# A two-layer float32 block on one Trainium2 core: the low part of every fourth pair of weight blocks formed by an accumulating DMA instead of VectorE

## Chip, cores and metric

One Trainium2 chip, one core of it. The metric is the device time of one execution in microseconds (us), lower is better.

## What is computed

Two transformer layers on 256 tokens of width 2048, everything in float32. Layer 1 is a hybrid mixer (an indexed sparse attention with 8 heads and a block attention with 8 heads, merged by two sigmoid gates), a cross attention to 256 memory rows, and a SwiGLU feed-forward of width 5632, each followed by residual and layer norm. Layer 2 has three attention branches of 4 heads (forgetting, chunked with relative positions, stick breaking), each with a silu gate, an up-projection and a sigmoid gate of width 2048, and an output product. By far the most of the work is the products with weight matrices:

```
x = layer_norm(ALPHA * x + hybrid_mixer(x, ...), ...)
x = layer_norm(ALPHA * x + mem_cross_attention(x, mem, ...), ...)
x = layer_norm(ALPHA * x + swiglu(x, w_ffn_in, w_ffn_out), ...)
x = hybrid_layer(x, norm_g, w_in, ...)      # layer 2
```

## The kernel before

**Products.** TensorE multiplies float32r operands, a form with a shorter mantissa. To keep float32 results, every operand is written as a sum of two parts, hi and lo, and three products are summed: hi by hi, hi by lo, lo by hi (`mm3`, L121 to L126: L124 and L126 read the weight's hi, L125 its lo). The activations, transposed, are the stationary operand (128 x 128), the weights the moving one (128 x 512).

**Weights.** `load_w` (L105 to L119) brings the weights in as pairs of blocks of 128 rows: a tile `raw` of 128 x 2 x 512 float32 (512 KB) by a DMA of SyncE's queue (L112), then `split` (L100 to L102): ScalarE copies raw into `hi` with a cast to float32r (L101), VectorE subtracts hi from raw into `lo` (L102).

```
    def split(src, hi, lo):
        nc.scalar.copy(hi, src)
        nc.vector.tensor_sub(lo, src, hi.bitcast(F32))
```

`raw`, `hi` and `lo` come from three rings of six buffers each (N_R = 6 and N_W = 6). So the cast of a pair waits until TensorE has read the pair six places before it, and the load of a pair until VectorE (and ScalarE) have read the raw six places before. 760 pairs go through `load_w`. The first 24 are those of the indexer queries (w_qi, 16) and of the narrow panel w_misc (8, 336 columns). All later ones have 512 columns, and every product takes a multiple of eight pairs, or four in w_oa, w_ob, w_up and each of the two halves of w_kvm for the values of the memory.

**Order of the products.** `gemm_panels` (L128 to L150) goes block by block over k: for each block both token tiles, three matmuls each, so 12 matmuls per pair. Where a layer norm follows (w_out, w_omem, the last group of w_fo) and in the last product (w_out2), the last TAIL = 8 blocks (four pairs) go token tile by token tile: first all eight blocks for tile 0, then all eight for tile 1. After a layer norm (w_qmem, the first w_fi, the first w_qkvg) the first HEAD = 8 blocks do the same.

**Other work on the engines involved.** ScalarE also evacuates PSUM, does exponentials, sigmoids and squares. VectorE also does layer norms (`layer_norm_T`, L528 to L548), softmax pieces, gates and `ln_affine` (L550 to L559), which multiplies and adds rows of gain and offset to x. GpSimd (POOL) makes a few masks at the start and issues the DMAs of its own queue: broadcast rows of 512 columns into tiles `bb` (three buffers, `bias_tile`, L95 to L98, issued at L93), x itself (L501), the relative-position tables (L799, L800) and some small constants. The framework plans the order on each engine by costs of its own, so an engine's order is not the order of the text: three `bb` loads and the small constants stand at the start of POOL's queue, for instance. Once planned, each engine and each queue goes in order.

Of the kernel before, what the change touches and what calls it, by code (L numbers as in the profile page):

```python
# [11 lines left out]
OP = mybir.AluOpType  # L12
# [20 lines left out]
N_EARLY2 = 2  # L33
E1 = 1

# columns of w_in
C_QD, C_KV, C_QI, C_KI, C_WI, C_QM, C_KM, C_VM, C_GA, C_GB = (
# [3 lines left out]
def build(ctx, tc, nc, a):  # L41
# [27 lines left out]

# [1 line left out]
    ident = const.tile([128, 128], F32, name="ident")  # L71
# [4 lines left out]
    nc.vector.memset(eps6, EPS)  # L76
    # token tile 1 sees 256 keys; the tables of tile 0 are the right halves of its
    dist1 = const.tile([128, 256], F32, name="dist1")
# [21 lines left out]
    def split(src, hi, lo):  # L100
        nc.scalar.copy(hi, src)  # L101
        nc.vector.tensor_sub(lo, src, hi.bitcast(F32))  # L102

# [1 line left out]
    def load_w(chunk_ap, kn, n, pieces=1):  # L105
        """One chunk of weights: kn blocks of 128 rows, n columns; hi and lo parts of each."""
        parts = []
        for k0 in range(0, kn, 2):
            raw = raws.tile([128, 2, n], F32, name="raw", tag="raw")
            for i in range(pieces):  # L110
                q = slice(2 * i // pieces, 2 * (i + 1) // pieces)
                nc.sync.dma_start(raw[:, q, :], chunk_ap[:, k0 + q.start:k0 + q.stop, :])  # L112
            hi = his.tile([128, 2, n], F32R, name="hi", tag="hi")
            lo = los.tile([128, 2, n], F32R, name="lo", tag="lo")
            for i in range(pieces):
                q = slice(2 * i // pieces, 2 * (i + 1) // pieces)
                split(raw[:, q, :], hi[:, q, :], lo[:, q, :])
            parts += [(hi[:, i, :], lo[:, i, :]) for i in range(2)]
        return parts  # L119
# [8 lines left out]
    def gemm_panels(panels, n=512, head=0, tail=0):  # L128
        """panels: (w_ap, acts, evac) each; acts: list over k of (hi, lo) [128, 256];
        w_ap: [chunks, 128, 4 * n]. The first `head` and the last `tail` blocks of 128 rows  # L130
        go token tile by token tile, the others block by block."""
        items = [(p, k) for p, (_, acts, _) in enumerate(panels) for k in range(len(acts))]
        cut = len(items) - tail
        groups = ([items[:head]] if head else []) + [[i] for i in items[head:cut]] + ([items[cut:]] if tail else [])
        pss, w = {}, {}
        for g in groups:
            for p, k in g:
                if (p, k) not in w:
                    ap = panels[p][0]
                    for i, part in enumerate(load_w(ap[k // 4].rearrange("p (k n) -> p k n", n=n), 4, n)):  # L140
                        w[p, k + i] = part
            for tt in range(2):
                for p, k in g:
                    _, acts, evac = panels[p]
                    if (p, tt) not in pss:
                        pss[p, tt] = ps_g.tile([128, 512], F32, name="ps_g", tag="ps_g")[:, :n]
                    last = k == len(acts) - 1
                    mm3(pss[p, tt], acts[k], w[p, k], tt, k == 0, last)
                    if last:
                        evac(tt, pss[p, tt])  # L150
# [10 lines left out]
    def transpose4(src):  # L161
        """src [128, 512] -> PSUM [128, 4, 128], each block of 128 columns transposed."""
        pt = ps_t.tile([128, 4, 128], F32, name="ps_t", tag="ps_t")
        for i in range(4):
            nc.tensor.transpose(pt[:, i, :], src[:, i * 128:(i + 1) * 128], ident)  # L165
        return pt
# [26 lines left out]

# [1 line left out]
    def scores(q, k, tt, w):  # L195
# [20 lines left out]
    def weigh(ps, v, causal_keys=True):  # L216
        """ps: per token tile [128, 2, 256]; v(i, sc) -> [128 keys, 128]. PSUM [128, 2, 256] = out^T."""
        o = ps_a.tile([128, 2, 256], F32, name="ps_a", tag="ps_a")
# [16 lines left out]

    # =========================== layer 1: mixer ===========================
    def stream_parts(src, name, panels, first=False):
        """Products with src^T (256 columns) that is loaded chunk by chunk beside the weights:
        a function that does the chunks from c0 to c1."""
        pss, loaded = {}, {}  # L240
# [6 lines left out]
        def part(c0, c1):  # L247
            for c in range(c0, c1):
                w0 = {}

                def first_w(i):
                    # between the pieces of src^T: blocks 2 i' and 2 i' + 1 of the first panel
                    if i % 2 == 0:
                        ap = panels[0][0][c].rearrange("p (k n) -> p k n", n=512)
                        w0[i // 2] = load_w(ap[:, i:i + 2, :], 2, 512, 2)
# [27 lines left out]
    def warm(func, after):  # L283
        """Has the function's table loaded once `after` is there, before it is needed."""
        nc.scalar.activation(small([128, 1], "warm"), after, func, bias=eps5, scale=0.0)
# [69 lines left out]

    # keys of the memory
    kmemT = unit([128, 4, 256], F32, "kmemT")
    stream(a["memT"], "memT", [(a["w_kvm"][0], into_T(kmemT))])

    # indexer scores and the choice of 64 keys  # L360
    mdsa = []
    for tt in range(2):
        w = 128 * (tt + 1)
        acc = later(f"score{tt}", FLOOR, tt=tt)
        for bp in range(4):
            # blocks 2 bp, 2 bp + 1 of two heads each; the heads of one row half share a bank
            for half in range(2):
# [20 lines left out]

    # keys and values of the latent attention, per head
    def load_pairs(ap):  # L390
# [111 lines left out]

    # residual + layer norm
    stats = {}
# [14 lines left out]

    # gains and offsets of the layer norms with one column per block of 128 of x's columns  # L520
    def columns(name):
# [6 lines left out]
    def layer_norm_T(g, b, prs, warm_up):  # L528
        """For a token tile: x becomes (x - mean) / deviation; prs get its transpose with gain and offset."""
        def ln(tt):  # L530
# [19 lines left out]
    def ln_affine(i, then=None):  # L550
        """Gain and offset on x itself."""
        for j in range(4):
# [8 lines left out]
    mA = acts_of(mT)  # L561
    # values of the memory: the first chunks run beside the layer norm
    vmem = unit([128, 2, 512], F32, "vmem")
# [5 lines left out]

    # =========================== memory attention ===========================  # L570
    v_part(0, V_CUT)
# [29 lines left out]

    # =========================== feed forward ===========================
    x2A = acts_of(x2T)
# [41 lines left out]

    # The rms norm's factor of a token, r3, is a factor of the token's rows of all products with
    # w_in_2: it comes in after them. hn here is x3 norm_g.

    # =========================== layer 2 ===========================
    hA = acts_of(hnT)  # L650
# [4 lines left out]

    # the branch gates of the first branch; its rows wait for r3
    first = []
# [16 lines left out]

    # silu of the branch gates, transposed
    sgT = []
# [14 lines left out]

    # log of the forget gates and its running sum
    fraw = const.tile([128, 16, 4], F32, name="fraw")
# [20 lines left out]
    nc.scalar.activation(fe, fe, AF.Exp)  # L714
    # log(1 + e) = log(u) e / (u - 1) with u = 1 + e rounded, and e where u = 1
    nc.vector.tensor_scalar(fu, fe, 1.0, None, op0=OP.add)
# [56 lines left out]

    # branch a: forgetting attention
    qT = proj_norm_T(a["w_qkvg"][0, 0], 0)
# [20 lines left out]

    # branch b: chunked attention with relative positions
    rb = [unit([128, 4, 128 * (tt + 1)], F32, f"rb{tt}") for tt in range(2)]
# [21 lines left out]

    # branch c: stick breaking
    qT2 = proj_T(a["w_qkvg"][2, 0], hA, sc=r3)
# [16 lines left out]
    for tt in range(2):  # L839
# [4 lines left out]
        for h in range(4):  # L844
            # softplus(z), then its sum over this key and the later ones
            nc.vector.scalar_tensor_tensor(e[:, h, :], z[:, h, :], 0.0, e[:, h, :], op0=OP.max, op1=OP.add)
            sr = tmp([128, 256], "scan")
            nc.vector.tensor_tensor_scan(sr[:, 0:w], e[:, h, ::-1], e[:, h, ::-1], 0.0, OP.add, OP.bypass)
            nc.vector.tensor_sub(z[:, h, :], z[:, h, :], sr[:, w - 1::-1] if w == 256 else sr[:, 127::-1])
    # gates and up-projections  # L850
    def gate2(n, j):
# [40 lines left out]

# [1 line left out]
def _panels(w, n=512, kc=4):  # L894
    """[K, N] -> [N / n, K / (128 kc), 128, kc * n]"""
    k, m = w.shape
# [4 lines left out]
def _lay_out(i):  # L901
# [13 lines left out]
    o["w_gb"] = _panels(w[:, C_GB:])  # L915
    # [h, d, c] -> [128 c, 2, (h d)];  [h, c, d] -> [128 c, 2, (h d)]
    o["w_ukT"] = np.ascontiguousarray(f["w_uk"][0].reshape(8, 128, 2, 128).transpose(3, 2, 0, 1)).reshape(128, 2, 1024)
# [45 lines left out]
```

## Time and profile before

| | us |
|---|---|
| span of the profiled execution, first to last instruction | 2244.9 |
| median of the timed runs | 2246.86 (two: 2244.22 and 2249.5) |
| TensorE busy | 2217.8 (99%) |
| VectorE busy | 1278.9 (57%) |
| ScalarE busy | 1056.4 (47%) |
| GpSimd busy | 36.8 (2%) |
| DMA, mean rate | 189 GB/s |

The page gives the profiled execution's span, not its time as the other runs are timed. The median of the timed runs is 1.96 us above the span. A busy TensorE in this profile means that a matmul was under way; matmuls overlap, so a row's mean duration is longer than the step from one matmul to the next.

### The profile page before, as it was taken

How to read it: one execution, taken by the hardware profiler on the slowest of the kernel's cores; microseconds unless marked ns; L12 is line 12 of the kernel's file. 1: busy time of each engine (PE TensorE's matmuls, PEld its weight loads, DVE VectorE, ACT ScalarE, POOL GpSimd, SP SyncE). 2: the span in 40 equal slices, each digit the busy share in tenths (PEclk: the TensorE clock that was granted, in tenths of full speed). 3: DMA queues.
4: the chain of work that ended last, by engine and by line, in shares of the span. 5: the costliest groups of instructions: out<-in, count | busy, mean ns of one | idle time of the engine just before them, and what ended most of it. 6: DMA issues, size and time to landing. Idle time of an engine off the chain costs nothing.

```text
span 2244.9 us, 26525 instructions
## 1 busy us (share of the span) xinstructions
PE 2217.8 (99%) x10080; PEld 1819.9 (81%) x10080; DVE 1278.9 (57%) x1563; ACT 1056.4 (47%) x1327; POOL 36.8 (2%) x75
## 2 busy tenths in 40 slices
PE   8999999999999999999999999999999999999999
PEld 6788888888887788888888888887788888888887
DVE  5666455555558774454455545467565565655553
ACT  5655445444435554443344434446555554444442
POOL 1000000000000000000000000001000000000000
PEclk9999999999999999999999999999999999999999
DMA  7654555656766375555555556557455556666563
GB/s 275 206 166 144 183 174 171 200 194 199 249 196 197 132 236 191 191 188 192 193 188 188 190 194 194 187 173 229 144 173 175 165 169 203 197 204 199 191 201 115
DMA packets 118480, 423.96 MB, mean 189 GB/s; under 512 B 13728, under 2 KB 14288, under 8 KB 118352
## 3 DMA queue, kind: packets, MB, share of 16 engines
q1 hardware_dynamic: 113760, 407.59, 55.2%
q0 software_dynamic: 4592, 14.68, 2.4%
q8 instruction: 79, 1.29, 0.2%
q14 instruction: 49, 0.40, 0.1%
HBM read 420.11 MB, written 2.10 MB: 188 GB/s over the span
## 4 chain that ended last, share of the span: by engine, by line
issue 66%; PE 30%; DMA 2%; POOL 1%; DVE 1%; ACT 0%; POOLq 0%; DVEq 0%; ACTq 0%
PE ps_g L125 9%; PE ps_g L126 9%; PE ps_g L124 9%; DMA bb<-ln_b 1%; PE ps_t L165 1%; DMA bb<-ln_g 1%; POOL bb L93 0%; DMA bb<-b_gate 0%; PE ps_a L198 0%; PE ps_a L232 0%; DVE lo L102 0%; PE ps_a L233 0%; ACT tmp L298 0%; PE ps_t L221 0%; PE ps_a L741 0%
## 5 line engine op out<-in xcount | busy, mean ns | idle before, releaser
L102 DVE TENSOR_TENSOR lo<-raw,hi 128x1024 fp32r<-128x1024 f32 (+2 forms) x766 | 931.7, 1218 | 874.7 <-ACT hi L101 873.7
L101 ACT CAST hi<-raw 128x1024 fp32r<-128x1024 f32 (+2 forms) x766 | 802.5, 1049 | 1038.4 <-PE ps_g L126 995.9
L125 PE MATMUL ps_g<-lo,hnTh 128*128 128x512 f32 x768 | 301.8, 393 | 2.3 <-DVE lo L102 2.3
L126 PE MATMUL ps_g<-hi,hnTl 128*128 128x512 f32 x768 | 302.1, 393 | 0.0
L124 PE MATMUL ps_g<-hi,hnTh 128*128 128x512 f32 x768 | 302.1, 393 | 0.0
L124 PE MATMUL ps_g<-hi,x2Th 128*128 128x512 f32 x704 | 275.0, 391 | 0.0
L126 PE MATMUL ps_g<-hi,x2Tl 128*128 128x512 f32 x704 | 274.8, 390 | 0.0
L125 PE MATMUL ps_g<-lo,x2Th 128*128 128x512 f32 x704 | 274.2, 390 | 0.0
L124 PE MATMUL ps_g<-hi,xTh 128*128 128x512 f32 (+1 forms) x608 | 236.5, 389 | 6.2 <-ACT hi L101 6.2
L125 PE MATMUL ps_g<-lo,xTh 128*128 128x512 f32 (+1 forms) x608 | 236.9, 390 | 1.5 <-DVE lo L102 1.3
L126 PE MATMUL ps_g<-hi,xTl 128*128 128x512 f32 (+1 forms) x608 | 237.8, 391 | 0.0
L125 PEld LDWEIGHTS ps_g<-lo,hnTh 128*128 128x128 f32 x768 | 145.1, 189 | 32.3 <-DVE lo L102 2.7
L124 PEld LDWEIGHTS ps_g<-hi,hnTh 128*128 128x128 f32 x768 | 145.2, 189 | 29.7 <-ACT crow L742 0.3
L126 PEld LDWEIGHTS ps_g<-hi,hnTl 128*128 128x128 f32 x768 | 144.9, 189 | 29.5
L125 PEld LDWEIGHTS ps_g<-lo,x2Th 128*128 128x128 f32 x704 | 132.2, 188 | 27.3 <-DVE lo L102 0.2
L124 PEld LDWEIGHTS ps_g<-hi,x2Th 128*128 128x128 f32 x704 | 132.2, 188 | 27.2 <-DVE x2Th L546 0.2
L126 PEld LDWEIGHTS ps_g<-hi,x2Tl 128*128 128x128 f32 x704 | 132.2, 188 | 27.1
L124 PEld LDWEIGHTS ps_g<-hi,xTh 128*128 128x128 f32 x608 | 114.7, 189 | 28.9 <-ACT hi L101 6.9
L126 PE MATMUL ps_g<-hi,hTl 128*128 128x512 f32 x352 | 137.3, 390 | 0.0
L124 PE MATMUL ps_g<-hi,hTh 128*128 128x512 f32 x352 | 137.2, 390 | 0.0
L125 PE MATMUL ps_g<-lo,hTh 128*128 128x512 f32 x352 | 136.9, 389 | 0.0
L125 PEld LDWEIGHTS ps_g<-lo,xTh 128*128 128x128 f32 x608 | 114.6, 188 | 25.6 <-DVE lo L102 3.4
(325 smaller groups left out, 2403.3 us busy)
## 6 DMA issues: line engine op xcount, KB each, us to landing
raw<-w_fi SPq DMA_DIRECT2D x176, 512.0 KB, 4.1
raw<-w_qkvg SPq DMA_DIRECT2D x96, 512.0 KB, 3.7
raw<-w_g SPq DMA_DIRECT2D x96, 512.0 KB, 4.4
raw<-w_fo SPq DMA_DIRECT2D x88, 512.0 KB, 3.7
raw<-w_out SPq DMA_DIRECT2D x64, 512.0 KB, 4.5
raw<-w_ga SPq DMA_DIRECT2D x32, 512.0 KB, 4.7
raw<-w_gb SPq DMA_DIRECT2D x32, 512.0 KB, 4.6
raw<-w_up SPq DMA_DIRECT2D x24, 512.0 KB, 4.6
```

The costliest lines, as they stand in the source:

```text
L101: nc.scalar.copy(hi, src)
L102: nc.vector.tensor_sub(lo, src, hi.bitcast(F32))
L124: nc.tensor.matmul(ps, ah[:, tok(tt)], wh, start=first, stop=False)
L125: nc.tensor.matmul(ps, ah[:, tok(tt)], wl, start=False, stop=False)
L126: nc.tensor.matmul(ps, al[:, tok(tt)], wh, start=False, stop=last)
L165: nc.tensor.transpose(pt[:, i, :], src[:, i * 128:(i + 1) * 128], ident)
```

## The change

A constant DMA_LO = 4 and a second way to split are added. From the 25th pair on, every fourth pair that `load_w` loads in one piece with 512 columns takes it: ScalarE copies raw into hi as before, then writes the negated raw, rounded to float32r, into lo, and a DMA of GpSimd's queue adds raw onto lo in place. VectorE has no part in such a pair. The pairs meant are those numbered 28, 32, ..., 760: (760 - 28) / 4 + 1 = 184 of them. The pairs are still counted over all of `load_w`; the activations' splits are as before. The diff also takes out comments and docstrings, which is left out here.

```
+DMA_LO = 4
...
+    pairs_done = [0]
+
+    def split_dma(src, hi, lo):
+
+        nc.scalar.copy(hi, src)
+        nc.scalar.mul(lo, src, -1.0)
+        nc.gpsimd.dma_start(lo, src, accum_op=OP.add)
+
     def load_w(chunk_ap, kn, n, pieces=1):
...
             hi = his.tile([128, 2, n], F32R, name="hi", tag="hi")
             lo = los.tile([128, 2, n], F32R, name="lo", tag="lo")
+            pairs_done[0] += 1
+            by_dma = pieces == 1 and n == 512 and pairs_done[0] > 24 and pairs_done[0] % DMA_LO == 0
             for i in range(pieces):
                 q = slice(2 * i // pieces, 2 * (i + 1) // pieces)
-                split(raw[:, q, :], hi[:, q, :], lo[:, q, :])
+                (split_dma if by_dma else split)(raw[:, q, :], hi[:, q, :], lo[:, q, :])
```

## Rows read from the trace of the kernel before

**Rows 1.** The page: busy time of each engine, TensorE's granted clock by slices.

```profile
PE 2217.8 (99%) x10080; PEld 1819.9 (81%) x10080; DVE 1278.9 (57%) x1563; ACT 1056.4 (47%) x1327; POOL 36.8 (2%) x75
...
PEclk9999999999999999999999999999999999999999
```

**Rows 2.** Windows: stretch, its us, busy per engine (instructions), clock, DMA share, GB/s.

```profile
0.00:100.00 100.00, 89.10 (x423) 72.84 (x423) 57.75 (x85) 58.34 (x85) 9.19 (x26) 1.00 0.77 263
100.00:200.00 100.00, 98.99 (x500) 80.25 (x500) 72.94 (x167) 55.69 (x98) 0.00 (x0) 1.00 0.45 144
700.00:800.00 100.00, 92.36 (x414) 73.57 (x413) 77.40 (x122) 57.00 (x99) 5.48 (x10) 0.97 0.53 170
900.00:950.00 50.00, 50.00 (x226) 41.39 (x225) 24.45 (x22) 21.15 (x23) 0.00 (x0) 1.00 0.60 189
1500.00:1550.00 50.00, 47.27 (x217) 37.48 (x216) 40.92 (x69) 35.58 (x72) 7.51 (x12) 0.97 0.58 177
1550.00:1700.00 150.00, 149.23 (x697) 119.46 (x696) 83.03 (x118) 79.34 (x109) 0.00 (x0) 0.99 0.51 174
```

**Rows 3.** Waits of TensorE: who waited for whom, us in total, times, longest.

```profile
PE ps_g L124 <- ACT hi L101: 6.2, 2, 5.3
PE ps_a L198 <- ACT prob L584: 3.8, 1, 3.8
PE ps_g L125 <- DVE lo L102: 3.6, 4, 2.3
```

**Rows 4.** Groups by line and shape: busy us, mean ns, idle before and its releaser.

```profile
L102 DVE TENSOR_TENSOR lo<-raw,hi 128x1024 fp32r<-128x1024 f32 x754 | 921.8, 1224 | 856.6 <-ACT hi L101 855.5
L101 ACT CAST hi<-raw 128x1024 fp32r<-128x1024 f32 x754 | 794.0, 1055 | 1026.4 <-PE ps_g L126 989.4 <-issue 8.6 <-ACT g L871 8.2
...
L871 ACT ACTIVATE g<-g 128x1024 f32<-128x1024 f32 x12 | 12.6, 1053 | 0.0
```

**Rows 5.** Timeline in the feed-forward, one pair: start us, us, engine, line, operation.

```profile
1005.07 0.39 PE L124 MATMUL ps_g<-hi,hTh 128*128 128x512 f32 x1
...
1005.27 1.05 ACT L101 CAST hi<-raw 128x1024 fp32r<-128x1024 f32 x1 [1.50 <-PE ps_g L126]
1005.30 0.39 PE L125 MATMUL ps_g<-lo,hTh 128*128 128x512 f32 x1
...
1006.36 1.23 DVE L102 TENSOR_TENSOR lo<-raw,hi 128x1024 fp32r<-128x1024 f32 x1 [1.28 <-ACT hi L101]
...
1007.99 1.05 ACT L101 CAST hi<-raw 128x1024 fp32r<-128x1024 f32 x1 [1.67 <-PE ps_g L126]
```

**Rows 6.** GpSimd's loads of x at L501: issue time of one in ns, landing.

```profile
L501 POOL DMA_DIRECT2D x<-x x4: 530/533/536, 575.9 to 577.5; - x4
...
DMA to landing us min/median/max: 8.1/11.1/14.2
```

**Rows 7.** GpSimd's broadcast rows at L93 (256 KB each): landing, all of them.

```profile
DMA to landing us min/median/max: 3.5/5.2/10.7
```

**Rows 8.** The page: DMA queues (packets, MB, share of 16 engines' span), one kind of issue.

```profile
q1 hardware_dynamic: 113760, 407.59, 55.2%
q0 software_dynamic: 4592, 14.68, 2.4%
...
raw<-w_fi SPq DMA_DIRECT2D x176, 512.0 KB, 4.1
```

**Rows 9.** Waits of SyncE's queue: us in total, times, longest.

```profile
SPq L112 <- DVE lo L102: 1706.0, 713, 10.4
```

**Rows 10.** Timeline at the end: the last pair's cast, the last matmul.

```profile
2224.58 1.05 ACT L101 CAST hi<-raw 128x1024 fp32r<-128x1024 f32 x1 [1.67 <-PE ps_g L126]
...
2240.47 0.39 PE L126 MATMUL ps_g<-hi,mT2l 128*128 128x512 f32 x1
```

**Rows 11.** Timeline of GpSimd in an `ln_affine` and in layer 2's gates.

```profile
799.60 0.54 POOL L93 DMA_DIRECT2D bb<-ln_g  x1 [8.27 <-DVE x L557]
...
2065.89 0.54 POOL L93 DMA_DIRECT2D bb<-b_gate  x1 [26.66 <-DVE g L467]
```

## Prediction

> **What bounds the kernel now.** I read the page's busy times first. TensorE is busy for 2217.8 of 2244.9 us, at a granted clock of nine tenths or more in each of the 40 slices, while VectorE has 1278.9 and ScalarE 1056.4 [rows 1]. All the time in which TensorE does nothing is therefore 2244.9 - 2217.8 = 27.1 us, 1.2% of the span. That is the most that faster work on any other engine could return, and it is under 2%, which is about what a measurement of this kernel can tell from no change.
>
> Then I looked at where the 27.1 us lie, by windows. 10.9 stand in the first 100 us, 1.0 in the next, 7.6 around the memory attention (700 to 800), 2.7 and 0.8 around layer 2's start; the 4.1 that are left are the evacuation and store after the last matmul. In the feed-forward (900 to 950) TensorE is never idle [rows 2]. Its waits name ScalarE's cast (6.2 us) and softmax (3.8) before VectorE's subtraction (3.6) [rows 3].
>
> Last the two engines that feed TensorE. VectorE's subtraction of a pair takes 1224 ns and ScalarE's cast 1055 ns; the idle time before the cast, 989.4 us of it, ends with L126, that is with TensorE giving a buffer back [rows 4]. Both are ahead of TensorE and wait for it. The timeline shows how far ahead: casts start at 1005.27 and 1007.99, so a pair takes 2.72 us and a matmul 2.72 / 12 = 0.227; TensorE starts the next pair at 1005.07 as the cast begins; VectorE starts its subtraction 0.04 us after the cast ends [rows 5]. With six buffers, five pairs lie between the cast of a pair and its first matmul: 5 x 2.72 = 13.6 us. The lo part is needed one matmul later, at 13.8, and is there after 1.05 + 0.04 + 1.23 = 2.3. It has 11.5 us in hand.
>
> **The change part by part.**
>
> *Removed from VectorE:* 184 subtractions of 1.224 us, 225 us of its busy time [rows 4]. In the steady stretches VectorE waits for casts that wait for TensorE, so this returns nothing there. What it can return lies where TensorE idles after the 24th pair: 1.0 + 7.6 + 2.7 + 0.8 = about 12 us at the very most [rows 2], of which only a part waits for VectorE.
>
> *Added to ScalarE:* 184 multiplications 128 x 1024 from SBUF to SBUF. The trace has the same form in the sigmoid on g, 1053 ns, and the cast, 1055 [rows 4]; I take 1.05. That is 193 us more, 1056 to about 1250, 56% of the span. In a steady stretch four pairs last 10.9 us and ScalarE would have 5 x 1.05 = 5.3 of casts and multiplications in them; the cover is its wait for TensorE. Where TensorE waits for ScalarE each multiplication could cost its full 1.05. The idle stretches after pair 24 (100 to 200, 700 to 800, 1500 to 1700) are 400 us long and hold 400 / 10.9 = 37 such pairs, so 39 us at most. With the 12 us from VectorE the net is between -12 and +39. As a multiplication only matters where it stands just before a waited-for instruction, and each takes an equally long subtraction off VectorE, I take +2.
>
> *Added to GpSimd and the DMA engines:* 184 issues and as many accumulating transfers of 512 KB within SBUF. No row shows one. Call L the time from GpSimd's issue to the landing. The lo part of such a pair is then ready at 1.05 + 1.05 + 0.04 + L after the start of the cast, and must be there at 13.8: **L may be 11.7 us** before TensorE waits in a steady stretch. The nearest rows are GpSimd's loads of x, also 512 KB in rows of 4 KB: 8.1, median 11.1, 14.2, where the four were issued within 1.6 us, so that only the 8.1 had nothing of its own queue ahead of it [rows 6]. Half the size takes 3.5 to 10.7, median 5.2 [rows 7]; on SyncE's queue 512 KB take 4.1 [rows 8]. The ends are 3.5 and 14.2; I take 8.1, the row of equal size with an empty queue. It leaves 3.6 us.
>
> *Where the lead is shorter:* in the four tails the last four pairs are needed at half the distance. At the end the last cast starts at 2224.58; the tail is 48 matmuls of 0.227 before 2240.9, so it starts at 2230.0, and the last pair's lo is needed 18 + 1 matmuls later, at 2234.3 [rows 10]. L may be 2234.3 - 2224.58 - 2.14 = 7.6 us there. All panels hold four or eight pairs, so the last pair of each tail has a number divisible by four and goes by DMA. At L = 8.1 each tail waits 0.5 us: 4 x 0.5 = 2. In the three heads the eighth pair gets the second's buffer after 8.2 of the head's 10.9 us and may take L = 9.0: no cost.
>
> *Moved: the release of raw.* SyncE's loads now wait for VectorE's subtraction, 1706 us in 713 waits, so they too are issued as early as a buffer comes free [rows 9]. After the change every fourth buffer is free only at 2.14 + 8.1 = 10.2 us after its cast began, not 2.3. The next load into it lands 4.1 later [rows 8], at 14.3, and its cast is due at 6 x 2.72 = 16.3: 2 us to spare. The three loads queued behind it in SyncE's order start late as well, in a bunch; TensorE would see a late cast only after the further 11 us of lead. I count nothing; if L is above 10.2 the cast starts late, which shortens that lead.
>
> *DMA engines:* 55.2% of the span for 407.59 MB is 3.04 us of all engines per MB; GpSimd's queue has 2.4% for 14.68 MB, 3.67 us per MB [rows 8]. In four pairs (10.9 us) the loads take 4 x 0.524 x 3.04 = 6.4 us, and one more 512 KB at the dearer rate 1.9: 8.3 of 10.9, or 76%. An addition has to read the destination as well: at twice the price 10.2, 94%. Still under the 10.9, but close.
>
> The Trainium skill (Collectives: The Full Stack, section "The bandwidth ceiling: the fold count and why AG ≠ RS ≠ AR") speaks against the change: a DMA that adds runs at half the rate of a copy since it reads two sources. No run here has shown it. By it the 94% and the longer L of the first rival hold; by the plain copy row, 76% and L = 8.1.
>
> **Sum:** 2244.9 + 2 (stages) + 2 (tails) = 2249 of span, and with the 1.96 us by which the median of the timed runs lies above the span, **2251 us**, +0.2%.
>
> **The rivals.**
>
> *Landing too late.* The mechanism is the lead of five pairs. From L = 11.7 TensorE waits at every fourth pair. Between the buffer's release and the need lies one other pair of the kind, whose wait lengthens the lead, so the wait is s = (L - 11.7) / 2 and the price 184 s. For it: from 256 KB (5.2) to 512 KB (8.1) the rows add 2.9 us; reading twice would be 1 MB, 8.1 + 2 x 2.9 = 13.9, so s = 1.1 and 202 us. Against it: in the burst of x loads a further 512 KB added only (14.2 + 1.6 - 8.1) / 3 = 2.6, so 10.7, within the lead; and source and target are both in SBUF. With L = 13: s = 0.65, 120 us, **2370** (2295 at L = 12.2, 2450 at 13.9).
>
> *DMA engines full.* If an accumulation costs three times a copy or more, four pairs need 6.4 + 5.7 = 12.1 us of DMA in 10.9, loads come late and TensorE waits 1.2 us per four pairs: 184 x 1.2 = 230, **2480**. The decisive point is a factor of 2.35. For it: nothing but the unknown; against it: the copy rows.
>
> *GpSimd's order.* Its queue also holds `bb` loads that wait for VectorE, 8.3 us in an `ln_affine`, 26.7 in the gates [rows 11]. An accumulation queued behind one waits as long. Before, nobody but `bb` stood there. If the order puts one behind such a wait in each of three `ln_affine` stretches: 3 x 8.3 = 25 us, **2274**. Against it: the order is planned, and the loads' releases and the pairs follow the same TensorE.
>
> *Relief.* If VectorE is what holds the memory attention and layer 2's start, the 12 us shrink and nothing else is paid: about **2240**. Against it: the waits named there are mostly ScalarE's [rows 3].
>
> **How the numbers follow.** Forecast 0.54; landing too late 0.22; DMA full 0.08; GpSimd's order 0.07; relief 0.09. Only relief is below 2244, and it can't reach 2% (2202): 0.02 for faster is left for what I have not seen. Slower by over 2% (above 2292) is the second and third case: 0.29 with a little of either end. Within 2%: 0.69. The range goes from relief, 2238, to 2400, inside the first rival: above it lie the DMA case and a third of late landing, 0.15, below some 0.03. The likeliest case alone would be 2244 to 2262 (L up to 11.1 makes each tail cost 3.5).
>
> **What would show it.** VectorE's busy time falls to about 1055 us, ScalarE's rises to about 1250, GpSimd's issues grow by 184. The landing time of `lo` is the number that decides: below 7.6 even the tails are free, up to 11.7 the steady stretch is, and above it L125 shows waits for that DMA 184 times. The DMA share in the feed-forward goes from 0.60 to some 0.75; at 0.95 and over the second rival is at work. The prediction is wrong if TensorE's busy windows between 850 and 1500 are no longer full.

## The result, and the profile after

The changed kernel takes 2276.08 us (median of two runs, 2275.71 to 2276.45) beside 2246.86 before: a ratio of 1.0128, 95% interval 1.0099 to 1.0158. It is slower by 29 us, inside the 2% that was taken as the bound of what counts, inside the range of the prediction, and well above its 2251.

The page of the changed kernel first: busy times, GpSimd's DMA queue, and the new kind of issue (KB each, median us to landing). They answer to [rows 1] and [rows 8]. In this kernel's listing the three matmuls are L135 to L137, VectorE's subtraction L103, the cast L102 or, in the new path, L110, the multiplication L111, the accumulating DMA L112.

```profile
span 2274.0 us, 27039 instructions
...
PE 2225.0 (98%) x10080; PEld 1822.2 (80%) x10080; DVE 1057.0 (46%) x1379; ACT 1222.7 (54%) x1511; POOL 197.3 (9%) x259
...
q0 software_dynamic: 31088, 111.16, 24.0%
...
lo<-raw POOLq DMA_DIRECT2D x184, 512.0 KB, 8.5
raw<-w_fi SPq DMA_DIRECT2D x176, 512.0 KB, 6.7
```

The span grew by 29.1 us. TensorE's idle time is span less busy: 2274.0 - 2225.0 = 49.0 us, where it was 27.1. So 21.9 us are new idle time. The other 7.2 us are in its busy time, though it ran the same 10080 matmuls: somewhere they took longer. VectorE lost 222 us of work and none of that came back.

The next view is the windows, in the order of [rows 2]: us, busy time per engine (instructions), clock, DMA share, GB/s.

```profile
600.00:650.00 50.00, 46.51 (x202) 38.00 (x201) 23.16 (x27) 23.99 (x27) 3.51 (x4) 0.97 0.93 304
700.00:750.00 50.00, 36.17 (x159) 27.99 (x158) 29.46 (x50) 25.93 (x49) 7.50 (x11) 0.88 0.77 231
800.00:850.00 50.00, 47.76 (x217) 38.86 (x216) 31.16 (x41) 29.12 (x38) 9.02 (x13) 1.00 0.88 262
850.00:1500.00 650.00, 648.19 (x2894) 535.60 (x2893) 253.75 (x240) 323.71 (x335) 49.94 (x58) 1.00 0.84 235
1500.00:1600.00 100.00, 92.00 (x412) 73.28 (x411) 53.60 (x81) 60.61 (x100) 12.19 (x16) 0.98 0.81 239
```

650 us of feed-forward hold about 60 of the 184 accumulations and lost 1.8 us. The same windows before had TensorE full from 600 to 650, from 800 to 850 and from 850 to 1500, and 43.13 and 97.27 us busy in the other two. The new idle time is therefore 3.5 + 7.0 + 2.2 + 1.8 + 5.3 = 19.8 of the 21.9 us, and nearly all of it stands in four places: the mixer's output product with the first loads of memT, the memory attention, the start of the feed-forward, and the start of layer 2.

The waits of TensorE (who waited for whom, us, times, longest) name two new causes beside those of [rows 3]:

```profile
PE ps_g L136 <- DMA lo<-raw: 13.3, 7, 3.5
PE ps_g L135 <- ACT memTh L102: 9.5, 1, 9.5
```

Only seven matmuls waited for an accumulation to land, out of 184 accumulations. The longest single wait is for something that the change does not touch: the cast of a chunk of memT.

Six of the seven stand in the four places named above. In four of these (7.2 of the 13.3 us) the accumulation landed within 4.7 to 6.7 us of its issue, so it was not slow: it was begun late. The longest wait shows how. The lines are ScalarE, TensorE, and the window over the load that came late:

```profile
619.99 1.14 ACT L102 CAST memTh<-memTraw 128x512 fp32r<-128x512 f32 x2 [8.87 <-DMA memTraw<-memT]
...
632.61 0.80 PE L136 MATMUL ps_g<-lo,mTh 128*128 128x512 f32 x1 [3.49 <-DMA lo<-raw]
...
600.00:620.00 20.00, 20.00 (x92) 16.60 (x91) 4.87 (x5) 6.12 (x8) 0.89 (x1) 1.00 1.03 371
```

ScalarE sat 8.87 us before a chunk of memT that took 13.8 us to land (5.4 before). So the multiplication of the pair that TensorE needed next began only at 624.92, and its accumulation, 6.3 us after its issue, landed too late. While memT was under way, from 606 to 620, the DMA engines were full: a share of 1 means that all 16 are busy (the records overshoot it by 3%), and the same window before had 0.72. Weight loads, an accumulation and GpSimd's four loads of x ran together there. The loads of x went out at 594 us, 18 later than before, with two accumulations ahead of them in GpSimd's queue.

How the standstill of 9.5 us came about can be read off four timelines of the changed kernel, in the order GpSimd, SyncE, ScalarE, TensorE:

```profile
727.64 0.54 POOL L94 DMA_DIRECT2D bb<-ln_g  x1 [2.94 <-DVE x L568]
728.48 0.91 POOL L112 DMA_DIRECT2D lo<-raw  x1 [0.30 <-issue]
...
715.13 24.52 SPq L121 DMA_DIRECT2D raw<-w_omem  x7
739.70 0.42 SPq L192 DMA_DIRECT2D memTraw<-memT  x1
...
723.74 1.06 ACT L111 ACTIVATE lo<-raw 128x1024 fp32r<-128x1024 f32 x1 [1.44 <-PE ps_g L136]
745.77 1.14 ACT L102 CAST memTh<-memTraw 128x512 fp32r<-128x512 f32 x2 [10.02 <-DMA memTraw<-memT]
...
746.44 0.80 PE L135 MATMUL ps_g<-hi,memTh 128*128 128x512 f32 x1 [9.51 <-ACT memTh L102]
747.03 0.63 PE L136 MATMUL ps_g<-lo,memTh 128*128 128x512 f32 x1
747.46 0.63 PE L135 MATMUL ps_g<-hi,memTh 128*128 128x512 f32 x1
```

ScalarE's multiplication is done at 724.80. GpSimd issues the accumulation at 728.48, since a load of `bb` that waited for VectorE stood before it. It lands 10.3 us later. Until then its raw buffer is held, and the waits of SyncE in this stretch have one of 10.0 us on it. The load of memT stands behind that weight load in SyncE's queue, and goes out at 739.70 (before, at 725.64). ScalarE, also in order, sits 10.02 us before the cast, with the softmax of the memory attention behind it. TensorE stands for 9.51 us. When it goes on, its matmuls soon start 0.43 us apart, not 0.227: the granted clock of this window is half, the 1.2 GHz level:

```profile
740.00:750.00 10.00, 3.56 (x9) 2.79 (x10) 2.64 (x7) 2.76 (x9) 0.00 (x0) 0.50 0.70 259
```

Part of the 7.2 us of longer busy time comes from this. The three longest of the new standstills (3.5, 9.5 and 3.2 us) came with a stretch at the lower level, those of 2.2 and 2.3 us did not. In all stretches at half the clock TensorE was busy for 18.3 us, and for 11.9 before. At the full clock the 6.4 us more would have taken half, so the clock accounts for about 3 us, an estimate from these two sums. Where the other 4 us of busy time lie is not shown.

Four queues, each in order, pass one late transfer on. That this chain ran is shown; whether removing one link saves it was the question for the experiments.

### The profile page after: what moved, and what is told of

Its sections match the earlier page's. It is cut to its first block, busy times and chain, and to the rows that moved or that the text cites. A ratio compares the mean times of both kernels' runs of the same rounds, so it can differ in the third digit from the quotient of the medians.

```text
span 2274.0 us, 27039 instructions
## 1 busy us (share of the span) xinstructions
PE 2225.0 (98%) x10080; PEld 1822.2 (80%) x10080; DVE 1057.0 (46%) x1379; ACT 1222.7 (54%) x1511; POOL 197.3 (9%) x259
## 4 chain that ended last, share of the span: by engine, by line
PE 82%; DMA 12%; DVE 2%; ACT 2%; issue 2%; SPq 0%; POOL 0%; ACTq 0%; DVEq 0%; POOLq 0%
PE ps_g L136 26%; PE ps_g L137 25%; PE ps_g L135 25%; DMA lo<-raw 4%; DMA raw<-w_fi 3%; PE ps_t L176 2%; DMA raw<-w_fo 1%; PE ps_a L209 1%; DMA bb<-ln_b 1%; DMA raw<-w_qi 1%; DVE lo L103 1%; PE ps_a L243 1%; DMA memTraw<-memT 1%; ACT hi L102 1%; ACT lo L111 1%
## 5 line engine op out<-in xcount | busy, mean ns | idle before, releaser
L103 DVE TENSOR_TENSOR lo<-raw,hi 128x1024 fp32r<-128x1024 f32 (+2 forms) x582 | 706.4, 1215 | 1082.6 <-ACT hi L102 1081.8
L102 ACT CAST hi<-raw 128x1024 fp32r<-128x1024 f32 (+2 forms) x582 | 607.3, 1045 | 678.6 <-PE ps_g L137 479.6
L112 POOL DMA_DIRECT2D lo<-raw x184 | 160.0, 869 | 1910.4 <-ACT lo L111 1696.5
L111 ACT ACTIVATE lo<-raw 128x1024 fp32r<-128x1024 f32 x184 | 195.3, 1061 | 218.1 <-PE ps_g L136 159.7
L135 PE MATMUL ps_g<-hi,hnTh 128*128 128x512 f32 x768 | 301.9, 393 | 0.3 <-DVE hnTh L557 0.3
L137 PE MATMUL ps_g<-hi,hnTl 128*128 128x512 f32 x768 | 301.5, 393 | 0.0
L135 PE MATMUL ps_g<-hi,x2Th 128*128 128x512 f32 x704 | 275.0, 391 | 0.0
L137 PE MATMUL ps_g<-hi,x2Tl 128*128 128x512 f32 x704 | 274.7, 390 | 0.0
L135 PE MATMUL ps_g<-hi,xTh 128*128 128x512 f32 (+1 forms) x608 | 237.3, 390 | 6.0 <-ACT hi L102 5.9
L137 PE MATMUL ps_g<-hi,xTl 128*128 128x512 f32 (+1 forms) x608 | 237.9, 391 | 0.0
L110 ACT CAST hi<-raw 128x1024 fp32r<-128x1024 f32 x184 | 189.9, 1032 | 3.4 <-PE ps_g L137 1.7
L135 PEld LDWEIGHTS ps_g<-hi,hnTh 128*128 128x128 f32 x768 | 145.0, 189 | 30.2 <-DVE hnTh L557 0.5
L137 PEld LDWEIGHTS ps_g<-hi,hnTl 128*128 128x128 f32 x768 | 145.1, 189 | 29.5 <-DVE hnTl L558 0.3
L135 PEld LDWEIGHTS ps_g<-hi,x2Th 128*128 128x128 f32 x704 | 132.2, 188 | 27.2 <-DVE x2Th L557 0.2
L137 PEld LDWEIGHTS ps_g<-hi,x2Tl 128*128 128x128 f32 x704 | 132.2, 188 | 27.0
L135 PEld LDWEIGHTS ps_g<-hi,xTh 128*128 128x128 f32 x608 | 114.9, 189 | 29.2 <-ACT hi L102 6.9
```

Source lines behind the costliest of these rows:

```text
L111: nc.scalar.mul(lo, src, -1.0)
L112: nc.gpsimd.dma_start(lo, src, accum_op=OP.add)
L135: nc.tensor.matmul(ps, ah[:, tok(tt)], wh, start=first, stop=False)
L137: nc.tensor.matmul(ps, al[:, tok(tt)], wh, start=False, stop=last)
```

## The experiments

Each ran beside the kernel before on the same chip; ratios are to those runs. Theories A to C were set first.

**Multiplication alone (mul_only).** The second line below stands in place of the DMA.

```
-        nc.gpsimd.dma_start(lo, src, accum_op=OP.add)
+        nc.vector.tensor_sub(lo, src, hi.bitcast(F32))
```

> ScalarE keeps the extra multiplication in all 184 pairs, but VectorE then forms lo as before; no accumulating DMA. Theory A (the raw buffer, held until the accumulation has landed, stalls SyncE's queue, and what is queued behind comes late): no such hold here, 2246 to 2252. Theory B (TensorE waits for the landing of lo itself): none here either, 2246 to 2252. Theory C (the 193 us of multiplications on ScalarE delay its other work): the change's loss stays, 2268 to 2276.

Measured: 2249.92 us, ratio 1.0014 (1.0005 to 1.0024). Theory C falls: 193 us more on ScalarE cost 3 us. The prediction's +2 for this term, which counted VectorE's relief as well, is about right.

**TensorE not waiting for the landing (no_lo_wait).**

```
-            parts += [(hi[:, i, :], lo[:, i, :]) for i in range(2)]
+            parts += [(hi[:, i, :], (hi if by_dma else lo)[:, i, :]) for i in range(2)]
```

> As the changed kernel, but in the 184 pairs TensorE reads hi where it should read lo, so that it never waits for an accumulation to land; the accumulations, the held raw buffers and the multiplications stay. The low parts of these pairs are left out of the product. Theory A: the 13 us of direct waits go, the wait behind the load of memT (9.5 us) and part of the lost clock stay, 2256 to 2268. Theory B: back to the kernel before, 2246 to 2253. Theory C: no change, 2272 to 2278.

Measured: 2272.31 us, 1.0112 (1.0097 to 1.0127). Theory B, as it was put, falls: without any direct wait of TensorE nearly 26 of the 29 us are still there. But the wait for the landing has not gone from the kernel. VectorE, which waits for no accumulation in the changed kernel, now waits for one before it can write into the same buffer of lo:

```profile
DVE lo L103 <- DMA lo<-raw: 157.3, 58, 4.3
```

So this run does not say what the loss would be with nobody waiting for a landing. (The product with hi is counted twice in these pairs, and the low part is left out.)

**Raw buffer free early (raw_free).**

```
-        nc.gpsimd.dma_start(lo, src, accum_op=OP.add)
+        nc.gpsimd.dma_start(lo, hi, accum_op=OP.add)
```

> As the changed kernel, but the DMA adds hi instead of raw onto lo: the same size and direction within SBUF, while raw is free as soon as ScalarE has read it. The low parts of these pairs come out as zero, so they are left out. TensorE still waits for the landing. Theory A: most of the loss goes, 2248 to 2258, SyncE waits for VectorE or ScalarE and no longer for the accumulation, and the load of memT in the memory attention is issued some 10 us earlier. Theory B: no change, 2270 to 2280. Theory C: no change, 2272 to 2278.

Measured: 2280.31 us, 1.0154 (1.0137 to 1.0171). Theory A, as I had put it, falls too. SyncE's waits no longer name the accumulation; the longest in total is this:

```profile
SPq L121 <- DVE lo L103: 1413.6, 540, 10.8
```

and memT goes out 6 us earlier, at 733.74, but TensorE's direct waits rise to 21.4 us. The held buffer was a link of the chain, not the cause of the loss by itself. When it was taken out, another wait took its place.

**memT on another queue (mem_act).**

```
-            nc.sync.dma_start(u[:, q, :], src[:, q, :])
+            (nc.scalar if name == "memT" else nc.sync).dma_start(u[:, q, :], src[:, q, :])
```

> As the changed kernel, but the loads of memT (8 of 512 KB) go through ScalarE's DMA queue, not SyncE's, so that they do not stand behind weight loads that wait for a held raw buffer. Theory A: ScalarE's wait for memT shrinks from 23 us to under 10, the 9.5 us of TensorE at the memory attention and the 3.5 us in the mixer's output product go with part of the lost clock, 2254 to 2264. Theory B: 2270 to 2278. Theory C: no change, 2272 to 2278.

Measured: 2269.26 us, 1.0099 (1.0074 to 1.0124), between the range of A and those of B and C. ScalarE's waits for memT fell from 23.2 to 17.0 us. The chain by way of memT may be worth some 7 us, but the interval overlaps that of the full change (1.0099 to 1.0158), so this is not clear of noise.

With C down, and neither A nor B enough by itself, the next question was where the loss lies and what it needs. Two runs split the 184 pairs by place.

**Only away from the stage changes (steady), and only at them (boundary).**

```
-            by_dma = pieces == 1 and n == 512 and pairs_done[0] > 24 and pairs_done[0] % DMA_LO == 0
+            by_dma = pieces == 1 and n == 512 and pairs_done[0] > 24 and pairs_done[0] % DMA_LO == 0 and not 192 < pairs_done[0] <= 272 and not 504 < pairs_done[0] <= 536
```

(and, for the other, the same two stretches without the "not", joined by "or").

> As the changed kernel, but the 28 pairs numbered 193 to 272 and 505 to 536 (the mixer's output product, the memory attention, the first panels of the feed-forward, its last product's end and the first panels of layer 2) are split by VectorE as before; 156 pairs keep the accumulating DMA. Theory D (the loss comes only where the lead of TensorE's buffers is short, around the layer norms and the memory attention): 2247 to 2255. Theory E (184 accumulations cost something wherever they are, by DMA traffic or by the planner's other order): 156 of 184 keep their share of the loss, 2268 to 2274.

> The reverse: only the 20 + 8 = 28 pairs numbered 193 to 272 and 505 to 536 that are divisible by four take the accumulating DMA, all others VectorE. Theory D: nearly the whole loss, 2265 to 2278. Theory E: 28 of 184 of it, 2248 to 2253.

Measured: 2258.42 us, 1.0055 (1.0040 to 1.0070), with 156 pairs, and 2262.80 us, 1.0071 (1.0051 to 1.0092), with 28. Over the 2246.24 of their kernel before that is 12.2 and 16.6 us, which add up to about the 29 of the full change. So neither D nor E stands alone, but per pair the places differ by a factor of about seven: 16.6 / 28 = 0.59 us against 12.2 / 156 = 0.08. In the feed-forward, 850 to 1500, the 156-pair kernel has TensorE busy for 649.98 of 650 us. Its longest new waits, 2.7 and 2.8 us, stand before gates (605 and 2082 us).

**Both waits taken away (traffic).** The edits of raw_free and no_lo_wait together.

> Both earlier edits at once: the DMA adds hi onto lo, so raw is free early, and TensorE reads hi where it should read lo, so that it never waits for the landing. The low parts of the 184 pairs are left out. What stays is the multiplications, the traffic of the accumulations and GpSimd's queue. If the direct wait and the held raw buffer each suffice alone for the loss (theory F): 2248 to 2256. If the traffic, which makes the weight loads land in 5 to 7 us instead of 4, or the planner's order carries it (theory E): 2266 to 2276.

Measured: 2274.09 us, 1.0121 (1.0104 to 1.0138). Theory F falls. But here too a buffer of lo that a DMA writes is not free for VectorE before the landing, read or not, and VectorE waits for it:

```profile
DVE lo L103 <- DMA lo<-hi: 202.3, 86, 4.1
```

The wait for the landing had moved, not gone, so the run can't say by itself what the traffic costs. The next two were built for that.

**The same waits, a short transfer (tiny).**

```
-        nc.gpsimd.dma_start(lo, src, accum_op=OP.add)
+        nc.gpsimd.dma_start(lo[:, 0, 0:64], src[:, 0, 0:64], accum_op=OP.add)
```

**The transfer, and nobody waiting for it (side).** On the kernel before, with VectorE forming every lo:

```
+    scratch = const.tile([128, 880], F32, name="scratch")
...
+            if by_dma:
+                nc.gpsimd.dma_start(scratch, hi.bitcast(F32).rearrange("p a b -> p (a b)")[:, 0:880], accum_op=OP.add)
```

> As the changed kernel, but the DMA adds only the first 64 columns of the first block of each of the 184 pairs (32 KB, not 512 KB); the rest of these pairs' low parts stays the negated raw and is left out. The multiplications, the 184 issues on GpSimd's queue, every wait for a landing and for the held raw buffer stay, only the transfer is short. Theory G (the length of the transfers and their traffic carry the loss): 2248 to 2254, landings of 3 to 5 us. Theory H (the planner's other order on the engines and the place in GpSimd's queue carry it): 2264 to 2276.

> The kernel before, all low parts formed by VectorE, no multiplication on ScalarE; besides, GpSimd adds 880 of the 1024 columns of hi onto a scratch tile by DMA for the same 184 pairs (440 KB each), and nothing waits for the scratch but the next such DMA. The waits of hi's buffers on these reads are long covered. If the traffic and the occupied GpSimd queue carry the loss by making the weight loads, memT and the broadcast rows late (theory G1): 2260 to 2274. If a pair has to wait for the landing for it to cost anything (theory G2): 2246 to 2253.

Measured: tiny 2248.87 us, 1.0010 (1.0000 to 1.0020); side 2257.46 us, 1.0045 (1.0030 to 1.0060). Tiny settles the first half. The multiplications, the 184 issues, their place in GpSimd's queue, the held buffers and the replanned order together cost 2 us, as long as the landing takes 3.0 us and not 8.5. Theory H falls: the other 27 us come with the size of the transfers, whatever the waits are by which they reach TensorE.

Side lies between the ranges of G1 and G2. It shows that traffic costs time even if TensorE waits for none of it: 86% of the bytes cost 11 us, about two fifths of the whole loss. In its feed-forward TensorE is full, with the DMA engines at 0.83. What is late is other transfers where something waits for them. VectorE's waits between 800 and 840 have one of 9.0 us for a row of gain; the second line is the window in which that row was issued:

```profile
DVE x L563 <- DMA bb<-ln_g: 9.0, 1, 9.0
...
800.00:810.00 10.00, 10.00 (x46) 8.28 (x45) 5.42 (x8) 4.42 (x7) 2.54 (x4) 1.00 1.03 321
```

The row landed 11.8 us after its issue. In the kernel before the wait was 3.1 us, the row took 6.3 us to land, and the same window had a DMA share of 0.85. In the feed-forward of side no 10 us are above 0.91. VectorE is in order, so the gate of the feed-forward (sg) behind it is late, and TensorE's transposes wait 4.6 us for it.

The other 18 us are a difference and not a measurement: side also leaves out the multiplications, moves fewer bytes, and its transfers land in 6.2 us at the median, not 8.5. What side does not have is anyone who waits for the landing of lo or of a held raw buffer. There the weight loads of the feed-forward land in 4.2 us, as before (4.1), and not in the changed kernel's 6.7. So it is not the traffic alone that makes those loads slow; the changed kernel issues them in bunches when a held buffer comes free (in the feed-forward four between 1005.24 and 1006.61, where side issues one every 2.72 us).

**A remedy for the late rows (after_bb4, before_bb4).** memT on ScalarE's queue, and a fourth buffer for `bb`; once in the changed kernel, once in the kernel before. A third run is the kernel before with memT alone (before_mem_act).

```
-    bbs = pool("bbs", 3)
+    bbs = pool("bbs", 4)
```

> The changed kernel with memT on ScalarE's DMA queue and a fourth buffer for the broadcast rows bb, so that VectorE waits less for rows of gain and offset that land late behind the accumulations. Theory G1+G2 (half the loss by late other transfers, half by pairs that wait for their landing): from the 2269 of memT alone to 2258 to 2266; VectorE's waits for bb fall from 19 us to under 10. If bb has no part in it: 2267 to 2272.

> The kernel before with the loads of memT on ScalarE's DMA queue instead of SyncE's, and no other change. If SyncE's order delays memT in the kernel before too (ScalarE waits 11.8 us for it): 2240 to 2246, TensorE's idle time between 720 and 740 falls from 6 us to about 3. If it is the chain of softmax on VectorE and ScalarE that sets that stretch: 2245 to 2250.

> The kernel before with memT on ScalarE's DMA queue and a fourth buffer for bb; no accumulating DMA. VectorE waits 12 us for bb in the kernel before, TensorE is idle for 2.4 us beside the last of these. If those waits reach TensorE: 2238 to 2242. If they are covered: the 2242 of the kernel with memT alone, 2241 to 2244.

Measured: after_bb4 2265.48 us, 1.0088 (1.0072 to 1.0103). That is in the range of G, but its interval overlaps that of mem_act, and the waits for bb only fell from 19 to 12 us, so the share of bb in the changed kernel is not shown. Without the accumulations: before_mem_act 2242.37 us, 0.9984 (0.9975 to 0.9994), and before_bb4 2239.72 us, 0.9971 (0.9961 to 0.9982). Both beat the kernel before, by 4 and 6 us, and the changed one by over 30. Their intervals overlap, so the times alone do not show what the fourth buffer adds. In the profiles TensorE's idle time around the start of layer 2 (1530 to 1550) is 2.3 us in the kernel before, 2.4 with memT alone, and 0.4 with the fourth buffer.

## Why the prediction was right, and where it was off

The class and the sign were right: no change within 2%, a little slower, since TensorE was the bound and could return at most 27 us. The likeliest case was put at +4 us, with 2244 to 2262 as its own bounds, and came out at +29, outside them. That the whole range held is in part luck: its upper part stood for landings above 11.7 us as a rule, which did not come. Point by point:

- *VectorE's relief returns nothing.* Right: 222 us of work gone (225 forecast), no stretch clearly faster.
- *ScalarE's multiplications, 1.05 us each, cost +2.* Right: 1061 ns each, +3 us for them alone (mul_only), +2 with VectorE relieved (tiny). ScalarE's busy time rose to 1223 us and not to 1250; in the records neighbouring instructions overlap by some 0.1 us (the multiplication above ends at 724.80, the cast behind it starts at 724.71).
- *L = 8.1 us against a lead of 11.7 in the steady stretch.* Right: median 8.5, between 4.5 and 12.1, and the feed-forward lost 1.8 us. The rival "landing too late" needed more than 11.7 as a rule and did not come: 7 waits, 13.3 us, not 184. The one wait for an accumulation in the steady stretch, 0.6 us, followed a landing of 12.1 us, about as a lead of 11.7 has it. By the letter, though, the forecast's sign of being wrong did show: 850 to 1500 was no longer quite full.
- *The tails, 4 x 0.5 us, and the heads, nothing.* The sum is near, the parts are not: one tail (of w_fo) waited 2.3 us after a landing of 9.3, the other three not at all, and one head (of w_qmem) 1.3 us after a landing of only 4.7.
- *GpSimd's order, 2274 us.* Within 2 us of the measured time, by luck. Its mechanism is in the chain above, at 728.48. But of the 184 accumulations only two were issued more than 2 us after the end of their multiplication (3.7 and 5.0 us; the median is 0.29), not three by 8.3, and tiny, which keeps such delays (3.0 and 2.2), loses 2 us.
- *Relief, 2240 us.* It did not come: no stretch got clearly faster.
- *DMA engines.* The accumulations took (24.0% x 2274.0 - 2.4% x 2244.9) / 96.5 MB = 5.1 us of all engines per MB, 1.4 times the loads of the same queue (3.67) and 1.7 times those of SyncE's (3.04), where "twice" the former was the upper of my two cases. No run has a plain copy within SBUF. The feed-forward's share went to 0.81 to 0.88 from 0.60, between the forecast 76 and 94%. The half rate, which the Trainium skill (Collectives: The Full Stack, "The bandwidth ceiling: the fold count and why AG ≠ RS ≠ AR") states for the adding step of a ring of cores, was too dear for this transfer. The factor of 1.4 is well short of the 2.35 at which the engines would be full on average.
- *"Moved: the release of raw ... I count nothing"* and the *"+2 (stages)"* of the sum: here the forecast failed. The mechanism was in it. It said that loads behind the held buffer start late, in a bunch, and that the stage changes are where time can be lost. But the lead of 11 us that was to cover it is that of the steady stretch. I had bounded the stages at -12 to +39 by ScalarE and VectorE alone and took +2. With the waits on transfers the term measured 20 us of new idle time, 7.0 of it in the memory attention behind a late load of memT.
- *Traffic as a price only when the engines are full.* I had asked this of the average over four pairs, and where that average holds it was right: side lost nothing in the feed-forward at 0.83. But at the stage changes several queues load at once. There the engines were full for 10 to 20 us (1.03 in the changed kernel from 600 to 620 and in side from 800 to 810), and single transfers came 5 to 8 us later to an engine with no lead.
- *The clock* was not in the sum: about 3 of the 29 us are matmuls at the lower level, by the estimate above.

What stays open: how the 18 us that side does not have divide between TensorE's direct wait, the held raw buffer with its bunched loads, and the rest of the traffic. Each edit that took one wait away let another grow or come up, such as VectorE's wait for a buffer of lo. tiny shows that they vanish together when the transfer is short.

## What to carry to other kernels

Work moved from an engine with time to spare to a DMA can be paid for by other transfers: count not only the bandwidth that is left on average, but the stretches where several queues load at once and an engine waits for a transfer with no buffer ahead of it. A lead worked out in the steady stretch does not hold at the changes of stage; there each in-order queue passes a late landing on to whatever stands behind it. Where TensorE is the bound, look for such a place first: in the kernel before another loading queue for memT and one more buffer for rows gave 6 us (0.3%), where 225 us less work on VectorE had given none.

## What the hardware showed that I had not expected

GpSimd needs 862 ns to issue an accumulation and 538 ns for a broadcast load in the kernel before; 184 such issues were harmless here (tiny). An accumulation of 512 KB within SBUF took 4.5 to 12.1 us to land, with a median of 8.5. That is not much quicker than GpSimd's loads of the same size from HBM, 8.1 to 14.2 in their burst [rows 6]. SyncE's weight loads of the feed-forward took 6.7 us to land beside the accumulations and 4.1 before. In side, where the traffic is much the same and no raw buffer is held, they took 4.2. TensorE's step of 0.43 us for the matmuls after a 9.5 us standstill, at a granted clock of 0.50, made the standstill dearer than its own length.
